# Modulation weights and their matmul visits moved from attention to the output projection, with attention's plan drawn anew

## The chip, the cores and the metric

The kernel runs on one core of one Trainium2 chip. The metric is the time of one execution on the device in microseconds, the median of several runs. Five engines work side by side, each through its own list of instructions in order: TensorE (PE, with its weight loads PEld), VectorE (DVE), ScalarE (ACT), GpSimd (POOL) and SyncE (SP), which issues nearly all DMA transfers here.

## The reference, cut to what matters

One layer of a diffusion transformer runs over 128 context tokens and 512 latent tokens with shared weights. Its second half is modulated by vectors that come out of the conditioning vectors `c` and `c_ctx`; their weights `w_ada` are what the change moves.

```python
ada_ctx = (jax.nn.silu(c_ctx) @ w_ada[i] + b_ada[i])[None, None, :]
ada_lat = (jax.nn.silu(c) @ w_ada[i] + b_ada[i])[:, None, :]
...
sh1, sc1, g1, sh2, sc2, g2 = jnp.split(ada, N_ADA, axis=-1)
u = rms_norm(h, p["g_pre1"]) * (1 + sc1) + sh1
mo, k, v = mixer(u, p, rope_tabs, ctx_k, ctx_v)
h = h + g1 * rms_norm(mo, p["g_post1"])
u = rms_norm(h, p["g_pre2"]) * (1 + sc2) + sh2
h = h + g2 * rms_norm(conv_ffn(u, p), p["g_post2"])
```

In `mixer`, attention has 16 query heads in four groups that share a key and value head each. Context tokens see only context tokens; latent tokens see all latent keys and 128 cached context keys, 640 in all. Its output is multiplied by `w_att_out` (1024 x 1024), which is the output projection of the change.

## The kernel before

All 640 tokens stay on the core. Every float32 operand of a large product is cut into a high and a low part ("hi" by ScalarE, "lo" by VectorE or GpSimd), and three matmuls replace one. Weights come as units of 512 KB into one of three `raw` buffers and are cut into one of three pairs `whi`, `wlo`. Units 8 to 15 are the query weights, two to each group; 16 and 17 are weights of two gates, 18 to 25 the eight column tiles of `w_att_out`.

Attention works in 36 steps, nine to a head group: one for the context tokens and two for each of four tiles of 128 latent tokens. `q_tile` makes the queries of one group and tile out of four pieces (`q00.0` and so on, line 689), which VectorE, ScalarE and GpSimd rotate and normalise, and which are turned on TensorE (line 1055). A step then runs as a chain:

- the scores `s` of two heads (line 1097, TensorE);
- their maximum (line 1144, VectorE), the exponential (line 1149, ScalarE), its high part `P1` (line 1155, ScalarE) and low part `P2` (line 1162 on VectorE for the first head; line 1160 for the second, on GpSimd where `POOL_WAY` has a 1, else on VectorE);
- a DMA transpose `T` of each head's parts, from `P` to `PT` (line 1166, or 1127 for the context step, SyncE);
- the product `pv` with the values (line 1191, TensorE), after a spreading of the inverse sums (line 1183);
- scaling and cutting of the result into `AH` and `AL`.

The order of all this is written out by hand. `work` names each piece of work with its engine, what it comes after and the buffers ("rooms") that it takes from a pool. `follow` then goes through the string `PLAN`: each item is the number of a piece, a letter for one of its ways (which engine does it), and digits that pick its buffers. Each engine, SyncE included, gets its instructions in the order of the plan. Behind attention, TensorE, VectorE and ScalarE keep the order of the program, while the framework places SyncE's transfers itself, as soon as their buffers allow.

The modulation weights: `w_ada` of the second scale and part of the second shift come as ten loads of 512 KB. Two of them go to `AR`, memory that attention's output will use later; eight go through the `raw` ring between the units (`LOADS`). A visit multiplies two of these loads by the conditioning vectors: `ada2_mm` issues 16 small matmuls (line 288), and VectorE adds the result to `acc`, which lies in a table no longer needed (line 1014 for the first, 1016 for the others). There are five visits in attention (`VISITS`), and `ada2_fold` (lines 315 to 321) turns `acc` into columns of `mod`, read far later, in the feed-forward half.

The projection follows directly. Its loop has eight column tiles `j`; each takes a unit, cut two tiles ahead (`next_unit`, lines 198 and 199, loads at line 215), and runs 48 matmuls (lines 233 to 235) of 320 columns into two PSUM banks, `2j` and `2j + 1` modulo 8, by way of `plain_gemm`. Beside it, in tiles 0 to 5, the list `making` builds the right-hand operands `T1` to `T4` of the next stage, and tiles 6 and 7 begin the loads of the next stage.

Of the kernel before, what the change touches and what calls it, by code (L numbers as in the profile page):

```python
# [12 lines left out]
F32 = mybir.dt.float32  # L13
# [35 lines left out]
68a0 44a0 22a00 67a 2a1 11a 32a11 23a 122a 41a 69a 14a2 121a 3a 21a 33a 123a 15a 34a1 70a 12a22 4a 24a2 31a 42a30 0a 71a 16a 6a  # L49
45a 35a 80a1 73a0 1a4 36a 74a 72a0 81a 51a1 75a 5c0 82a 7a 8a3 43a 37c1 25a 83a 9a 46a 76b 38a4 86a1 10a 93a2 139a 26a 47b2  # L50
106a0 84a10 39a 27a3 87a 48a3 40a 94a 88a 13b 49a 28a1 50a 17a4 77a4 29a 95a 78a0 30a 52a3 140b 96a 53a 18a1 79a 99a0 141b 54a3
97a22 19a 367a2 55a 100a 85a 144a 108a2 368a 101a 58b4 56a3 369a 109a 20a 89a 57a 60a1 90a1 107a 110a 371a3 370a 91a1 124a3 372a
59a0 92a 373a5 111a 98a 125a 65a 63a 102a 379a21 112a01 184a 61a 66b 185a 114a2 103a0 380a 126a1 104a2 64b 115a 381a 385a 127a
116a 382a2 105a 128a 62a 386a0 383a 113a 374a0 145a 117a 390a 384a1 392a01 375a0 147b 387a1 376a 118a4 377a 393a 129a 388a 119a3
378a 394a 398a 142a0 132a1 146b 389a0 120a 399a1 143a 133a 130a12 134a 395a3 409a21 186a 403a 400a0 396a 131a 148a 215a 410a
397a2 135a 415a 411a 149a 217b 391a1 416a0 150a2 216b 151a0 420a 412a4 422a01 152a 401a 220a 417a2 413a 158a0 423a 414a3 418a
136a4 428a 159a 424a 402a4 137a0 160a 153a 429a1 138a 187a4 425a1 154a 433a 419a5 430a3 426a 155a3 161a 431a 156a1 188a 261a
157a 439a02 427a0 164a2 162a01 404a 440a 163a 432a1 445a 441a 171a0 165a 260a 446a0 166a 172a 405a0 450a 442a4 452a12 406a 167a
447a0 443a 173a 407a 448a 458a 444a2 168a2 174a 408a 169a2 453a 459a1 421a1 449a4 170a 177a1 454a 178a 469a20 175a12 179a 460a2
463a 189a0 455a1 470a 461a 434a 475a 471a 176a 462a3 456a 476a0 190a 180a 435a1 480a 472a3 482a10 436a 457a5 477a4 473a 191a  # L60
437a 478a 488a 474a0 499a2 438a 489a 483a 192a 479a1 500a 490a0 451a1 195a0 491a 501a 464a 193a20 492a2 196a 194a 484a 181a2
502a 202a0 197a 182a3 493a 503a2 183a 203a 485a1 198a 504a 465a2 486a 199a2 505a4 221a 204a 466a 511a21 200a0 223b 467a 201a
487a3 468a 205a 222b 512a 481a1 517a 208a2 262a 513a 206a01 518a1 209a 218a0 207a 514a3 522a 210a 524a01 291a 515a 211a 219a
519a4 516a5 530a 293b 212a4 525a 494a 531a 520a 213a1 532a0 224a 214a 495a0 292b 533a 521a0 526a 263a4 496a 527a2 535a 225a 296a
264a 497a 336a 528a 541a12 337a 227a1 498a 534a1 226a1 234a1 228a 547a 229a 529a2 523a0 542a 548a 230a 235a 543a 549a1 231a2
552a 236a 232a2 550a 544a3 237a 233a 551a3 545a 554a20 240a0 241a 238a22 546a0 536a 242a 560a 239a 247a1 555a 537a1 561a0 243a
538a 248a 556a 571a10 539a 565a 557a4 540a 562a0 244a0 558a 249a 245a3 563a 572a 559a5 250a 246a 573a 577a 553a0 564a1 253a2
578a1 254a 251a00 255a 574a2 584a20 582a 579a1 575a 252a 265a1 585a 256a 576a2 580a 590a 257a3 586a 266a 258a0 566a 591a0 259a
581a0 587a3 601a10 595a 567a2 588a 592a4 267a 607a 589a3 593a 602a 268a 608a1 568a 594a1 271a1 614a20 569a 269a11 603a 272a
278a1 270a 609a0 615a 273a 604a2 612a 570a 279a 620a 616a 274a 506a0 605a 297a 610a 280a 606a5 507a0 617a1 508a 631a1 298b 621a0  # L70
618a 281a 611a4 509a 632a 299b 622a3 643a02 510a 284a0 625a 633a 623a 338a 282a22 275a0 649a 596a1 283a 276a1 634a 285a 650a1
277a 583a 286a 619a1 644a 635a4 651a2 294a0 636a 287a 597a1 624a3 652a 645a 656a21 598a 599a 654a 895a 637a0 295a 600a 657a
646a0 288a1 897b 662a 300a 653a2 289a2 658a 290a 896b 301a 647a 663a 626a1 302a0 898a 659a1 667a 303a2 613a 660a 648a1 664a3
304a 638a0 665a 627a0 305a 661a3 673a02 628a 639a2 306a 629a 640a 630a 339a3 641a 666a4 679a 307a1 642a 680a0 340a 902a 655a0
674a 906a 308a3 681a4 309a 686a12 675a 682a 930a1 676a2 684a 687a 668a 683a5 692a 688a 310a1 677a 693a1 678a0 311a 669a1 697a
689a0 670a 703a02 694a1 690a 671a 695a 312a 691a1 709a 704a 313a 710a0 696a2 672a 705a 314a10 716a12 711a3 315a 714a 323a0 316a1
722a 712a 706a4 685a1 317a 723a 717a 318a 713a3 324a 707a 724a2 718a 725a 319a 698a 708a4 719a0 727a 320a2 699a2 720a 325a 726a0
321a0 700a 733a21 322a 701a 721a5 702a 326a 739a 715a1 734a 329a0 740a1 327a21 735a 746a01 330a 328a 741a1 744a 331a 341a0 736a3
747a 332a 728a 737a 748a 742a 752a 738a1 749a4 763a2 729a0 342a 750a 753a0 743a2 764a 333a2 754a2 343a 757a 730a 334a1 751a3
755a 765a 344a 335a 775a10 345a02 756a4 731a 766a 347a2 346a 732a 767a0 354a0 781a 348a 907a1 782a1 776a 349a 355a 768a 783a3  # L80
908a 350a 777a 769a0 788a02 784a 899a 786a 356a 778a1 789a 900b 785a5 909a 794a 790a 901b 357a 779a 795a0 910a 358a11 791a4
805a12 799a 360a1 359a 792a 911a 796a2 351a0 361a 811a 903a 758a1 797a 806a 352a2 745a 812a1 780a3 353a 904b 807a 818a02 905b
798a4 813a0 816a 912a0 808a3 824a 814a 759a0 793a1 819a 913a 825a0 809a 362a 820a 914a 815a2 760a 826a1 835a21 829a 363a 761a
827a 821a2 762a 915a 841a 787a1 822a 916a 842a1 836a 364a0 828a3 843a4 848a01 365a3 844a 837a 366a 800a 823a5 849a 838a0 846a
854a 917a0 850a 845a1 839a 801a2 918a 855a0 802a 919a 810a4 803a 865a21 859a 856a1 804a 851a2 857a 920a 866a 770a1 921a 871a
867a 830a0 858a0 852a 872a1 817a 868a4 876a 853a3 873a3 869a 878a01 831a1 874a 771a0 832a 840a5 772a 833a 922a2 884a 773a 879a
875a2 885a 923a 774a 880a 834a 860a1 870a4 886a1 889a 881a2 924a 887a 931a 882a 888a0 847a 925a 883a3 861a2 862a 877a0 863a 864a
926a 927a 890a 928a 891a1 892a 893a 929a 894a
"""
POOL_WAY = "11111110100111111011101111111110"  # L90
# [20 lines left out]
def trunk_layer(ctx, tc, x_prompt, x_sample, cache_k, cache_v, c, c_ctx, w_ada, b_ada, g_pre1, g_post1, g_pre2,  # L111
# [557 lines left out]
    AR = region(ra, "r2b", [2, 1024], F32, "AR")  # L669
# [57 lines left out]
    with tc.tile_pool(name="att", bufs=1) as at:  # L727
# [16 lines left out]
        acc = both[1].rearrange("p a d -> p (a d)")[:, 0:256]  # L744
# [40 lines left out]
        def load(key, pos):  # L785
            after = [w for w in raw_users.get(ring[-3], ())] if len(ring) >= 3 else []

            def do():
                if key[0] == "a":
                    ada2_load(key[1])  # L790
                else:
                    state["limit"] = key[1] + 1
                    fetch(key[1] + 1)
            ring.append(key)
            loaded[key] = work(f"load {key}", "SP", do, after)
# [183 lines left out]
        def first_step(g, t):  # L979
# [6 lines left out]
        LOADS = [("u", 10), ("a", 0), ("a", 1), ("u", 11), ("u", 12), ("a", 4), ("a", 5), ("u", 13), ("u", 14), ("a", 6), ("a", 7), ("u", 15),  # L986
                 ("u", 16), ("a", 8), ("a", 9), ("u", 17), ("u", 18), ("u", 19)]
        VISITS = [((2, 3), 2), ((0, 1), 4), ((4, 5), 11), ((6, 7), 20), ((8, 9), 29)]
        ada_first = [work("load AR", "SP", lambda: [ada2_load(2 + i, AR[:, i]) for i in range(2)])]
        kept = []  # L990
# [4 lines left out]

        def visit(us, n):
            after = []
            for u in us:
                if u in (2, 3):
                    after += ada_first  # L1000
                else:
                    if ("a", u) not in loaded:
                        load_next(("a", u))
                    after.append(loaded["a", u])
            host = Room(ANY)

            def mm():
                ada2_mm(us, at_bank(host))
            w = work(f"ada {us}", "PE", mm, after + kept[-1:], [host])

            def keep():
                p = at_bank(host, 128)
                if us[0] == 2:
                    V.tensor_copy(acc[:, 0:128], p)
                else:
                    V.tensor_tensor(out=acc[:, 0:128], in0=acc[:, 0:128], in1=p, op=ALU.add)
            kept.append(work(f"keep {us}", "DVE", keep, [w] + kept[-1:] + (k_ready if us[0] == 2 else []), [host]))
            for u in us:
                raw_users["a", u] = [w]

        visits = {v[1]: v[0] for v in VISITS}

        def q_tile(g, t):
# [1010 lines left out]
    us = []  # L2034
# [345 lines left out]
```

## Time and profile before

| | |
|---|---|
| median of 3 runs | 1105.28 us (1102.85 to 1105.73) |
| the profiled execution | 1106.97 us |
| its span in the profile | 1105.2 us |
| attention | about 55 to 260 us |
| the output projection | about 260 to 317 us |

A row of a stage gives its start and end, its length, then for each engine the busy time and the number of instructions, and last the granted clock of TensorE (1.00 is full), the mean busy share of the 16 DMA engines and what they moved. A row in order of time gives the start, the duration, the engine, the line, the operation, output and input by the program's names, and in brackets how long the engine had been idle and what ended that. A row of waits gives who waited for whom, the total, how many times and the longest. Matmuls overlap in TensorE's pipeline, so the distance between two starts tells what one costs, and not its duration. The profile shows `acc` under the name of its table, `tabk`.

### The profile page before, as it was taken

What the parts mean: (1) busy time and instruction counts of PE and PEld (TensorE: products, weight loads), DVE (VectorE), ACT (ScalarE), POOL (GpSimd) and SP (SyncE); (2) the same over time, 40 slices, a digit from 0 to 9 for tenths busy, and PEclk for the clock granted to TensorE, in tenths of its full rate; (3) what the DMA queues carried; (4) which work ended last, traced back from release to release, by engine and by line L of the source; (5) the groups of instructions that cost most, each with busy time, mean ns of one, the idle gap of its engine ahead of it and who ended that gap; (6) DMA issues with size and microseconds to landing.
All of it is one profiled execution on the core that took longest, in us unless ns stands there. A gap on an engine that the chain in (4) does not pass through costs nothing.

```text
span 1105.2 us, 20360 instructions
## 1 busy us (share of the span) xinstructions
PE 1078.5 (98%) x8133; PEld 1001.8 (91%) x8133; DVE 856.6 (78%) x1307; ACT 584.1 (53%) x1055; POOL 135.3 (12%) x168
## 2 busy tenths in 40 slices
PE   8999988989999999999999999999999999999997
PEld 6788877879999999999999789999999999998886
DVE  5698877875559889988578558898999989989544
ACT  5468767873335445445522356655465545556442
POOL 1087545540000000000000021000000000000001
PEclk9999989999999999999999999999999999999999
DMA  9759989993234333322354645234344333435722
GB/s 322 222 134 218 180 138 187 161 180 77 77 92 122 102 95 97 106 77 77 107 185 146 214 153 153 77 100 139 110 130 127 118 108 114 127 101 190 265 85 95
DMA packets 245613, 152.18 MB, mean 138 GB/s; under 512 B 94602, under 2 KB 224134, under 8 KB 245518
## 3 DMA queue, kind: packets, MB, share of 16 engines
q1 hardware_dynamic: 245406, 150.84, 50.6%
q8 instruction: 64, 1.05, 0.4%
q14 instruction: 31, 0.25, 0.1%
q10 hardware_dynamic: 112, 0.04, 0.0%
HBM read 117.39 MB, written 11.44 MB: 117 GB/s over the span
## 4 chain that ended last, share of the span: by engine, by line
PE 87%; DMA 4%; DVE 3%; ACT 3%; issue 1%; POOL 1%; SPq 0%; DVEq 0%; ACTq 0%; POOLq 0%
PE b L1300 46%; PE b L233 10%; PE b L235 10%; PE b L234 10%; PE s L689 3%; DMA PT<-P 3%; PE s L1097 2%; PE s L1191 1%; PE s L233 1%; ACT s L1149 1%; PE s L235 1%; ACT P L1155 1%; PE s L234 1%; PE s L464 1%; DMA XT<-in_x_sample_dram 1%
## 5 line engine op out<-in xcount | busy, mean ns | idle before, releaser
L1300 PE MATMUL b<-ZBr,whi 128*128 128x320 f32 x688 | 152.1, 309 | 0.0
L1300 PE MATMUL b<-MT,whi 128*128 128x320 f32 x608 | 134.2, 309 | 0.0
L1300 PEld LDWEIGHTS b<-ZBr,whi 128*128 128x128 f32 x688 | 115.0, 188 | 0.1
L1300 PE MATMUL b<-ZBr,wlo 128*128 128x320 f32 x344 | 106.1, 309 | 0.0
L1300 PEld LDWEIGHTS b<-MT,whi 128*128 128x128 f32 x608 | 101.6, 188 | 0.0
L1300 PE MATMUL b<-MT,wlo 128*128 128x320 f32 x304 | 94.0, 309 | 0.0
L1287 ACT ACTIVATE whi<-SUM 128x1024 fp32r<-128x1024 f32 x40 | 42.2, 1054 | 78.5 <-DVE SUM L1814 76.0
L1844 DVE SCALAR_TENSOR_TENSOR Y<-C,cffn,Y 128x642 f32<-128x642 f32 x88 | 77.6, 882 | 0.9
L199 DVE TENSOR_TENSOR wlo<-raw,whi 128x1024 fp32r<-128x1024 f32 (+1 forms) x31 | 34.2, 1102 | 50.2 <-ACT whi L198 49.9
L1300 PE MATMUL b<-ZBT,whi 128*128 128x320 f32 x320 | 71.1, 309 | 0.0
L1300 PE MATMUL b<-UL,whi 128*128 128x320 f32 x228 | 70.8, 311 | 0.0
L1300 PE MATMUL b<-UH,wlo 128*128 128x320 f32 x228 | 70.1, 307 | 0.0
L1300 PE MATMUL b<-UH,whi 128*128 128x320 f32 x228 | 69.7, 306 | 0.0
L1287 ACT ACTIVATE whi<-WB 128x1024 fp32r<-128x1024 f32 x38 | 40.1, 1054 | 55.3 <-DVE WB L1395 55.3
L1291 DVE TENSOR_TENSOR wlo<-raw,whi 128x1024 fp32r<-128x1024 f32 (+1 forms) x51 | 50.4, 1019 | 21.3 <-ACT whi L1287 21.3
L1300 PEld LDWEIGHTS b<-ZBr,wlo 128*128 128x128 f32 x344 | 64.6, 188 | 0.0
L1308 ACT ACTIVATE p<-b 128x320 f32<-128x320 f32 x78 | 34.2, 439 | 55.5 <-PE b L1300 53.6
L1300 PEld LDWEIGHTS b<-MT,wlo 128*128 128x128 f32 x304 | 57.1, 188 | 0.0
L1300 PEld LDWEIGHTS b<-ZBT,whi 128*128 128x128 f32 x320 | 54.3, 188 | 1.7
L1144 DVE TENSOR_REDUCE marks<-s 128x1 f32<-128x640 f32 x64 | 51.4, 816 | 4.7 <-PE s L1097 4.7
L1291 DVE TENSOR_TENSOR wlo<-WB,whi 128x1024 fp32r<-128x1024 f32 x38 | 46.5, 1223 | 8.7 <-ACT whi L1287 8.6
L1287 ACT ACTIVATE whi<-raw 128x1024 fp32r<-128x1024 f32 (+1 forms) x51 | 43.5, 892 | 17.6 <-PE b L235 10.4
(423 smaller groups left out, 3226.8 us busy)
## 6 DMA issues: line engine op xcount, KB each, us to landing
raw<-in_w_in_dram SPq DMA_DIRECT2D x48, 512.0 KB
RAW<-in_w_up_dram SPq DMA_DIRECT2D x40, 512.0 KB
raw<-in_w_down_dram SPq DMA_DIRECT2D x22, 512.0 KB
raw<-in_w_ada_dram SPq DMA_DIRECT2D x16, 512.0 KB
actd<-Y SPq DMA_DIRECT2D x18, 321.0 KB
XT<-in_w_ada_dram SPq DMA_DIRECT2D x9, 512.0 KB
raw<-in_w_att_out_dram SPq DMA_DIRECT2D x8, 512.0 KB
raw<-in_w_conv_out_dram SPq DMA_DIRECT2D x8, 512.0 KB
```

What stands on the lines that cost most here:

```text
L199: V.tensor_tensor(out=lo[:, :n], in0=raw, in1=hi[:, :n].bitcast(F32), op=ALU.subtract)
L233: PE.matmul(out, ah, bh, start=start, stop=False)
L234: PE.matmul(out, ah, bl, start=False, stop=False)
L235: PE.matmul(out, al, bh, start=False, stop=stop)
L689: PE.matmul(out, a, b, start=start and n == 0, stop=stop and n == 2, skip_group_check=True)
L1097: PE.matmul(o[h], q_of(hl, i, rows), kk[kx][rows, g, ks], start=m == 0, stop=m == 2, tile_position=(64 * h, 0), skip_group_check=True)
L1144: V.tensor_reduce(out=mk[:, h:h + 1], in_=s_of(), axis=AX.X, op=ALU.max, negate=True)
L1287: S.activation(to[0], raw, AF.Copy)
L1291: V.tensor_tensor(out=lo, in0=raw, in1=hi.bitcast(F32), op=ALU.subtract)
L1300: PE.matmul(out, p[:, ws], q[:, k, :], start=start and k == 0 and n == 0, stop=stop and k == 3 and n == 2, skip_group_check=True)
L1308: S.activation(t, pair[j][b], AF.Copy)
L1844: V.scalar_tensor_tensor(out=y, in0=crows(j)[i][:, d:d + NACT], scalar=cffn[:, 44 * d + o:44 * d + o + 1], in1=y, op0=ALU.mult, op1=ALU.add)
```

## The change

The ten loads and the five visits leave attention, and with them `AR`, `VISITS`, `visit` and the fold. They go to the loop of the projection: four loads are issued ahead of it, into the memory of `T4` and `T2`, which `right_of` now claims only when it fills it; a visit stands behind the matmuls of tiles 0 to 4, each of the first three followed by the two loads that the buffer just read can take; the fold stands behind tile 5. `acc` moves to the end of `WB`. Attention has 912 pieces of work in place of 932, and `PLAN` and `POOL_WAY` are new; in the new plan the remaining loads (units 10 to 19) stand at other places between the transposes.

```diff
 PLAN = """
-68a0 44a0 22a00 67a 2a1 11a 32a11 23a 122a 41a 69a 14a2 121a 3a 21a 33a 123a 15a 34a1 70a 12a22 4a 24a2 31a 42a30 0a 71a 16a 6a
...
+67a0 14a0 22a00 137a 2a1 131a 44a2 15a 23a 0a 68a 3a 203a 24a0 1a1 16a 34a1 25a 6a 11a 69a 35a 41a 32a21 4a 70a 12a32 31a 21a
...
-POOL_WAY = "11111110100111111011101111111110"
+POOL_WAY = "11111111101111111011111011111110"
...
-    AR = region(ra, "r2b", [2, 1024], F32, "AR")
...
-        acc = both[1].rearrange("p a d -> p (a d)")[:, 0:256]
...
-                if key[0] == "a":
-                    ada2_load(key[1])
-                else:
-                    state["limit"] = key[1] + 1
-                    fetch(key[1] + 1)
+                state["limit"] = key[1] + 1
+                fetch(key[1] + 1)
...
-        LOADS = [("u", 10), ("a", 0), ("a", 1), ("u", 11), ("u", 12), ("a", 4), ("a", 5), ("u", 13), ("u", 14), ("a", 6), ("a", 7), ("u", 15),
-                 ("u", 16), ("a", 8), ("a", 9), ("u", 17), ("u", 18), ("u", 19)]
-        VISITS = [((2, 3), 2), ((0, 1), 4), ((4, 5), 11), ((6, 7), 20), ((8, 9), 29)]
-        ada_first = [work("load AR", "SP", lambda: [ada2_load(2 + i, AR[:, i]) for i in range(2)])]
-        kept = []
+        LOADS = [("u", u) for u in range(10, 20)]
...
-        def visit(us, n):
...
-                for n in sorted(visits):
-                    if n <= first_step(g, t):
-                        visit(visits.pop(n), n)
...
-        work("fold", "PE", folded, kept[-1:], [fold])
...
-    for name, tag in (("T1", "r5a"), ("T2", "r5b"), ("T3", "r6a"), ("T4", "r6b")):
-        z = rb.tile([128, 2, 4, HT], F32R, tag=tag, name=f"M{name}")
-        TT["m" + name] = (z[:, 0], z[:, 1])
+    TAG = {"T1": "r5a", "T2": "r5b", "T3": "r6a", "T4": "r6b"}
+    ada_rooms = {}
+
+    def ada2_fetch(i):
+        h = i // 2 % 2
+        if i % 2 == 0:
+            ada_rooms[h] = rb.tile([128, 2, 1024], F32, tag=("r6b", "r5b")[h], name=nm("ada"))
+        ada2_load(i, ada_rooms[h][:, i % 2])
...
     def right_of(name, x):
-        hi, lo = TT["m" + name]
+        z = rb.tile([128, 2, 4, HT], F32R, tag=TAG[name], name=f"M{name}")
+        hi, lo = TT["m" + name] = (z[:, 0], z[:, 1])
...
+    acc = WB[:, 3200:3328]
+    for i in range(4):
+        ada2_fetch(i)
     for j in range(KT):
         unit = next_unit()
...
                 S.activation(MA[:, j, b0:b1], out, AF.Copy)
+        if j < 5:
+            p = ada2_mm((2 * j, 2 * j + 1), bank((2 * j + 4) % 8 if j else 2))
+            if j == 0:
+                V.tensor_copy(acc, p)
+            else:
+                V.tensor_tensor(out=acc, in0=acc, in1=p, op=ALU.add)
+            if j < 3:
+                for i in (2 * j + 4, 2 * j + 5):
+                    ada2_fetch(i)
+        elif j == 5:
+            ada2_fold(acc, bank((2 * j + 4) % 8))
```

More of the change, by code (lines that the diff above doesn't have):

```diff
@@ L48 @@
 PLAN = """
-68a0 44a0 22a00 67a 2a1 11a 32a11 23a 122a 41a 69a 14a2 121a 3a 21a 33a 123a 15a 34a1 70a 12a22 4a 24a2 31a 42a30 0a 71a 16a 6a
-45a 35a 80a1 73a0 1a4 36a 74a 72a0 81a 51a1 75a 5c0 82a 7a 8a3 43a 37c1 25a 83a 9a 46a 76b 38a4 86a1 10a 93a2 139a 26a 47b2
-106a0 84a10 39a 27a3 87a 48a3 40a 94a 88a 13b 49a 28a1 50a 17a4 77a4 29a 95a 78a0 30a 52a3 140b 96a 53a 18a1 79a 99a0 141b 54a3
-97a22 19a 367a2 55a 100a 85a 144a 108a2 368a 101a 58b4 56a3 369a 109a 20a 89a 57a 60a1 90a1 107a 110a 371a3 370a 91a1 124a3 372a
@@ L53 @@
[L53 to L88, printed above, removed]
+67a0 14a0 22a00 137a 2a1 131a 44a2 15a 23a 0a 68a 3a 203a 24a0 1a1 16a 34a1 25a 6a 11a 69a 35a 41a 32a21 4a 70a 12a32 31a 21a
@@ new lines @@
+33a 45a 79a1 72a0 51a0 5a0 80a 132a 13a 8a2 7a 73a 52a3 46a 81a 17b1 9a 53a 82a 134b 10a 54a3 71a0 85a1 92a2 133a 74a 55a 56a0
+83a11 209a 93a 75a 57a 42a42 84a 76a3 94a 77a0 58b1 26a 18a1 43b 95a 78a 19a 27a2 86a 347a2 20a 98a2 105a0 87a 348a 47b3 28a3
+349a 36a 106a 88b 59b3 89a1 107a 99a 37a4 90a1 350a 29a 91a 108a 96a20 351a0 60a4 30a 48a1 111a0 118a2 112a 97a 65a 352a 38a3
+49a 113a 66a 119a 353a5 63a 50a 61a 64b 120a 109a01 39a 138a 121a 40a 110a 359a21 62a 100a 124a1 204a 114b 140a 115a1 135a0 360a
@@ new lines @@
+101a 116a2 139b 117a 361a 136a 125a 365a 102a1 206b 275a 362a2 141a 122a12 103a3 366a0 142a 126a 104a 205a 354a1 144a2 363a 123a
+281a 367a4 372a01 143a0 127a 355a0 364a0 145a 356a 146a 128a4 378a 357a 151a0 129a0 147a 358a 379a1 152a 130a 368a 373a 389a21
+380a3 370a 374a 381a 369a1 148a1 395a 153a 375a1 390a 149a1 154a 382a2 396a0 376a 157a0 150a 391a 402a10 377a3 155a21 397a0 400a
+383a 156a 158a 371a1 392a2 408a 398a 403a 164a0 409a1 393a 159a 404a 399a4 165a 410a4 413a 419a02 160a 405a3 394a5 411a 384a
@@ new lines @@
+406a 425a 407a0 161a3 385a2 166a 420a 162a3 426a0 386a 167a 412a1 163a 387a 421a 432a21 388a 168a10 427a1 430a 401a1 169a 433a
+170a1 422a0 428a 438a 434a 177a0 423a 439a1 429a2 178a 171a 435a2 443a 172a 449a01 440a3 436a 424a3 173a 414a 455a 441a 437a4
+450a 456a0 174a4 179a 175a2 415a1 176a 457a4 180a 416a 442a5 462a12 417a 458a 181a02 451a 418a 183a2 463a 431a1 452a1 182a 459a0
+453a 464a 190a0 468a 465a0 454a1 479a0 184a 469a1 466a 444a 185a 480a 470a2 467a2 186a 491a21 473a 445a0 460a 481a 446a 471a
@@ new lines @@
+191a 497a 447a 482a 472a3 492a 192a 483a3 498a0 448a 193a 484a 493a 187a1 485a4 194a21 504a10 188a0 499a4 502a 189a 195a 196a0
+461a1 505a 500a 494a1 510a 506a 474a 495a 501a5 511a 207a0 197a 475a2 515a 198a 507a0 476a 496a0 208a 477a 508a 512a2 199a 478a
+210a 521a21 509a1 513a 276a 211a 486a1 527a 212b 514a2 200a2 487a0 522a 201a1 277b 213a 528a1 488a 202a 214a 489a 875a 278b
+529a3 490a 534a10 215a1 523a 530a 879a 216a1 503a1 532a 524a4 535a 531a3 540a 536a 516a 525a 541a0 223a0 217a 517a1 545a 218a
@@ new lines @@
+542a1 518a 551a20 526a4 519a 537a0 219a 520a 224a 557a 543a 220a1 552a 225a 558a1 538a 221a3 544a0 226a 559a2 222a 564a01 229a2
+560a 553a 539a5 227a02 533a1 565a 554a3 228a 570a 566a 561a1 236a0 555a 571a0 237a 230a 567a4 562a 575a 231a 581a21 556a2 572a1
+568a 232a 546a 582a 573a 569a3 587a 583a 233a2 238a 547a0 234a2 548a 588a1 239a 235a 574a4 549a 594a01 240a21 584a0 550a 589a2
+241a 585a 563a1 242a0 590a 595a 586a0 611a2 600a 596a 249a0 591a5 612a 601a0 576a 243a 597a3 592a 605a 244a 602a4 598a 250a
@@ new lines @@
+577a2 245a 613a 599a1 578a 623a10 603a 251a 579a 629a 615a1 604a2 580a 252a 630a1 616a 246a1 255a1 624a 617a3 636a20 247a0 631a0
+253a10 625a 632a 642a 593a0 626a2 248a 637a 606a 643a 254a 633a4 634a 256a 638a 627a 262a1 257a 607a1 647a 628a0 614a 644a3 608a
+263a 258a 609a 645a 639a4 259a3 264a 610a 260a1 646a5 640a 282a 618a0 261a 653a02 284a 641a1 619a2 620a 283b 265a 621a 659a 883a
+622a 660a0 654a 279a0 268a2 666a12 876a 266a00 269a 267a 655a 635a1 672a 270a 661a1 877a 648a 656a0 667a 271a 673a1 280a 878b
@@ new lines @@
+664a 657a 649a1 674a2 272a4 650a 658a2 285a 662a 273a3 651a 274a 668a 286a 652a 887a 675a 683a02 288a0 677a 663a3 669a3 287a2
+289a 295a1 684a 290a 888a0 689a 685a 291a 296a 676a0 670a 690a0 889a 686a4 694a 696a12 691a0 687a 671a4 692a 297a 697a 292a2
+702a 698a 298a 688a1 890a 293a2 299a12 699a1 294a 891a 301a1 300a 700a 703a1 693a5 308a1 302a 892a 707a 713a01 704a2 303a 678a0
+304a 719a 705a 714a 720a0 665a 701a0 715a 726a21 679a0 706a4 724a 716a3 680a 309a 732a 681a 721a4 682a 310a 733a 717a 722a 305a0
@@ new lines @@
+311a 727a 718a2 306a0 734a0 743a0 307a 314a2 735a 695a0 728a 723a3 312a01 729a1 708a 744a 313a 736a1 730a 745a 321a1 315a 737a
+755a12 316a 731a5 709a2 746a 747a2 710a 322a 317a 761a 711a 712a 323a 762a1 756a 318a0 324a 748a 763a3 319a1 768a20 749a0 764a
+325a20 757a 320a 327a0 766a 758a4 738a0 774a 326a 765a4 769a 775a0 725a 759a 770a 750a1 328a 760a1 739a1 779a 329a 771a0 740a
+785a01 751a2 772a 741a 330a 776a1 742a 773a5 331a4 791a 777a 334a0 332a3 786a 792a1 335a 333a 778a2 787a 752a 798a12 793a2 796a
@@ new lines @@
+336a 753a 804a 794a 880a 754a 337a 805a0 799a 881b 795a3 767a1 338a10 788a3 806a4 789a 882b 780a 340a1 800a 790a0 341a 807a
+815a20 781a1 809a 801a0 782a 893a0 342a 339b 808a1 783a 816a 884a 894a 821a 343a 817a 885b 784a 895a 822a1 802a 344a1 886b 896a
+818a1 803a4 826a 345a2 828a10 819a 823a2 346a 897a 820a2 824a 797a1 834a 829a 835a0 898a0 825a5 830a 845a20 836a3 839a 810a
+831a4 846a 837a 832a 847a 899a 851a 833a0 811a2 900a 848a0 812a 901a 852a1 849a 838a3 813a 858a10 856a 853a1 814a 902a 854a
@@ L89 @@
+850a1 827a1 864a 859a 865a 903a2 855a4 860a 840a 866a2 869a 861a4 867a 904a 841a1 862a 911a 868a2 905a 842a 843a 863a5 906a 844a
+857a0 907a 908a 870a 909a 871a0 872a 873a 910a 874a
 """
-POOL_WAY = "11111110100111111011101111111110"
+POOL_WAY = "11111111101111111011111011111110"
 def rope_tables():
@@ L994, in load_next @@
                 load(LOADS[len(ring)], len(ring) - 28 if len(ring) < 3 else -5 + 2 * len(ring))
-        def visit(us, n):
[L997 to L1021, printed above, removed]
         def q_tile(g, t):
@@ L1246, in trunk_layer @@
                 users_of.setdefault(17, []).append(glast)
-        fold = Room(banks(6, 7))
-        def folded():
-            ada2_fold(acc, at_bank(fold))
-        work("fold", "PE", folded, kept[-1:], [fold])
         work("sigmoid", "ACT", lambda: S.activation(warm, mhalf[:, 0:1], AF.Sigmoid), exps_all)
```

## Prediction

> **What bounds the kernel now.** I read the page first (busy shares, chain), then the table by stage, then TensorE in order of time where attention stands still, then SyncE's queue there.
>
> ```profile
> span 1105.2 us, 20360 instructions
> PE 1078.5 (98%) x8133; PEld 1001.8 (91%) x8133; DVE 856.6 (78%) x1307; ACT 584.1 (53%) x1055; POOL 135.3 (12%) x168
> PE 87%; DMA 4%; DVE 3%; ACT 3%; issue 1%; POOL 1%; SPq 0%; DVEq 0%; ACTq 0%; POOLq 0%
> ...
> 55.00:260.00 205.00, 187.91 (x2458) 165.05 (x2457) 159.01 (x345) 152.10 (x354) 115.99 (x113) 0.98 0.91 167
> 80.00:245.00 165.00, 149.56 (x2032) 131.07 (x2034) 128.05 (x279) 126.81 (x293) 95.07 (x93) 0.98 0.99 176
> 260.30:316.70 56.40, 56.39 (x384) 56.40 (x385) 32.03 (x29) 18.95 (x26) 0.00 (x0) 1.00 0.25 74
> ```
>
> The stage rows give start:end, length, busy time of PE, PEld, DVE, ACT and POOL, granted clock, share of the 16 DMA engines, GB/s. Over the whole program TensorE is the bound, at 98%. Attention (55 to 260) is the exception: TensorE idles 205.0 - 187.9 = 17.1 us there, VectorE and ScalarE are at 78% and 77% of the inner stretch, and the DMA engines at 0.99. The projection (260.3 to 316.7) is the reverse: TensorE never idles, the DMA engines are at 0.25. So the change takes work from a stage with four nearly full resources to one with a single full resource, and that one is TensorE. From 316.7 on the next stage is as full of matmuls; I let a shift at that point pass to the end unchanged.
>
> Where attention stands still:
>
> ```profile
> PE s L1191 <- DMA PT<-P: 9.7, 5, 3.2
> ...
> 138.23 0.28 PE L689 MATMUL s<-whi,UH 128*128 128x256 f32 x1
> ...
> 139.18 0.28 PE L689 MATMUL s<-whi,UL 128*128 128x256 f32 x1
> ...
> 144.31 1.81 PE L1191 MATMUL s<-PT,VV 128*64 128x128 f16 x30 [3.20 <-DMA PT<-P]
> ...
> 146.43 0.42 PE L689 MATMUL s<-wlo,UH 128*128 128x256 f32 x1
> ...
> 148.57 0.41 PE L689 MATMUL s<-whi,UL 128*128 128x256 f32 x1
> ...
> 185.56 1.03 PE L1191 MATMUL s<-PT,VV 128*64 128x128 f16 x30 [2.61 <-DMA PT<-P]
> ...
> 243.85 1.03 PE L1191 MATMUL s<-PT,VV 128*64 128x128 f16 x30 [2.39 <-DMA PT<-P]
> ...
> 140.00:150.00 10.00, 6.80 (x67) 6.04 (x65) 4.79 (x11) 3.43 (x8) 2.58 (x4) 0.66 0.78 126
> ...
> 180.00:190.00 10.00, 7.01 (x135) 5.79 (x132) 5.63 (x15) 4.79 (x11) 2.30 (x3) 1.00 1.14 196
> ...
> 240.00:250.00 10.00, 7.61 (x110) 6.83 (x112) 5.16 (x12) 6.66 (x16) 1.75 (x2) 0.83 1.16 188
> ```
>
> The one large wait is that of the values' product (L1191) for a transposed tile: five waits, 9.7 us, three of them long. They cost more than their length. Behind the first, eight matmuls that took 0.95 us before it (138.23 to 139.18, 0.119 each) need 0.214 each (ten in 146.43 to 148.57): TensorE runs at half clock from 144.3 to about 149.6, which loses 2.6 us. The window at 240 has 0.83 of the clock, a loss of 10 x 0.17 = 1.7. Behind the second the clock stayed at 1.00. The waits with their clock cost 9.7 + 2.6 + 1.7 = 14.0 us.
>
> What the transposes stand behind, in SyncE's queue:
>
> ```profile
> 85.75 1.37 SPq L1166 DMA_TRANSPOSE PT<-P  x1
> ...
> 132.95 1.24 SPq L215 DMA_DIRECT2D raw<-in_w_in_dram  x2
> 134.29 0.52 SPq L282 DMA_DIRECT2D raw<-in_w_ada_dram  x1
> 134.90 4.52 SPq L1166 DMA_TRANSPOSE PT<-P  x1
> ...
> 177.72 0.62 SPq L215 DMA_DIRECT2D raw<-in_w_in_dram  x1
> 178.51 2.28 SPq L1166 DMA_TRANSPOSE PT<-P  x1
> ...
> raw<-in_w_ada_dram SPq DMA_DIRECT2D x6, 512.0 KB
> raw<-in_w_att_out_dram SPq DMA_DIRECT2D x4, 512.0 KB
> PT<-P SPq DMA_TRANSPOSE x64
> ```
>
> A transpose takes 1.37 us to issue when the queue is clear, 4.52 behind three loads, 2.28 behind one. The first two long waits, at 144.3 and 185.6, follow exactly these two places; the third has no load near it. A load is 524,288 bytes. The projection's row moves 74 GB/s at a share of 0.25, so 296 GB/s when full, 1.77 us a load. Between 80 and 245 there are 16 loads (six of them moved by the change, four of w_att_out and six of w_in), 28.3 us; the other 0.99 x 165 - 28.3 = 135 us belong to 64 transposes, 2.1 us each. The six loads that leave free 6 x 1.77 = 10.6 us of a queue that is full. The page "DMA: Bandwidth & Descriptors" of the Trainium skill (Latency and other measured facts) gives 261 GB/s for a transpose; for its 327,680 bytes that is, as an estimate from that page, 1.26 us, and the DMA engines would be only two thirds full. The share of 0.99 speaks against it, and the measurement decides; what would follow if the engines do have room is the second rival.
>
> **The change part by part.** First what leaves attention.
>
> ```profile
> 180.68 1.08 PE L288 MATMUL s<-raw,s 128*32 128x128 f32 x32
> 181.70 0.44 PE L1055 MATMUL s<-ident,QF 128*128 128x128 f32 x2
> ...
> 187.60 0.41 PE L315 MATMUL s<-sel,tabk 128*128 128x32 f32 x2
> 187.94 0.44 PE L1183 MATMUL s<-ident,marks 128*64 128x128 f32 x4
> ...
> 188.05 0.17 DVE L319 TENSOR_TENSOR mod<-s,feat 128x16 f32<-128x16 f32 x1 [4.21 <-PE s L315]
> ...
> L1014 DVE COPY tabk<-s x1: 293/293/293, 78.8 to 78.8; 128x128 f32<-128x128 f32 x1
> ```
>
> A visit occupies TensorE from 180.68 to 181.70, 1.02 us; five are 5.1. The fold takes 187.60 to 187.94, 0.34. Work of 5.4 us leaves a TensorE that is 91% busy; between nothing (they sat in idle time) and 5.4 I take 5.4, because work stands directly before and behind each. VectorE loses five small sums and the fold, and with it the 4.2 us that it stood still for the fold while TensorE waited for a transpose. I count nothing for that: the same transpose held both. By the new plan's way letters it does six half cuts more and two P2 fewer, so it stays about as full.
>
> Second, the waits. I counted in both plans how many score steps stand between a step's scores and its values' product in TensorE's order. Before, ten steps from 10 to 32 have two or fewer (10 to 13, 18 to 20, 22 to 24) while others have up to eight; after, five have two (11, 18, 20, 27, 29) and nearly all others three or four. The waits at 144.3 and 185.6 belong to steps 11 and 19, both with two; the one at 243.9 to step 30, whose transpose stood behind one of step 32, and after stands in turn. The loads that remain also move: u13 to u15 go ahead of step 1's transposes, u16 and u17 behind step 11's transposes, u18 and u19 on either side of one of step 21; none waits for a buffer whose last cut stands behind it. Half of the short distances are gone, and I let half of the 14.0 go: -7.0. Bounds: all 14.0 go, or none.
>
> Against that, the softmax starts later: the last query tile of the first group now stands before step 1. Its 24 matmuls at 0.119 are 2.85 us, and the two visits that stood there, 2.04, are gone: +0.8. Attention: -5.4 - 7.0 + 0.8 = -11.6.
>
> Third, the projection. The visits come back one for one, 5.1, and the fold 0.34, on an engine with no idle time. New is a wait behind the first visit: its sum is copied out of bank 2, and the next tile's matmuls begin in that bank. The fold's row gives 188.05 - 188.01 = 0.04 us from TensorE's end to VectorE's start; a drain of 0.28, that hop twice and a copy of 0.29 make 0.65. TensorE stands for it; VectorE's next cut waits behind the copy, and it is needed only a tile later. Later visits use banks whose next tile is two tiles away, and the fold reads a sum finished a tile before: nothing. Together +6.1; bounds 5.4 and, with a 0.65 at each visit, 8.7.
>
> Fourth, the loads in the projection, at nothing:
>
> ```profile
> 250.75 3.10 SPq L1166 DMA_TRANSPOSE PT<-P  x2
> ...
> 257.33 1.01 PE L1191 MATMUL s<-PT,VV 128*64 128x128 f16 x30
> ...
> 260.31 0.38 PE L233 MATMUL b<-AHa,whi 128*128 128x320 f32 x1
> ...
> 291.46 22.90 SPq L1380 DMA_DIRECT2D raw<-in_w_in_dram  x4
> ...
> DMA  9995000000000000002699991000000000000006
> ```
>
> A tile of the projection is 56.4 / 8 = 7.05 us, so the first visit comes at 260.3 + 7.05 = 267.4. Its loads go to memory that attention's tiles hold, at worst until the last values' product ends, 258.3. The last line is the DMA share in 40 slices of 286 to 300: the load issued at 291.46 is over by slice 25, 294.8, 3.3 us later. Two loads from 258.3 land by 258.3 + 3.3 + 1.8 = 263.4, four microseconds early, room for two loads of w_att_out ahead of them. The later ones are issued two tiles before their visit, 14 us. On the queue they pass, a load that waits for a visit holds back loads of w_att_out, which are wanted a tile later still. The DMA engines go from 0.25 to 0.25 + 17.7 / 62 = 0.54. The four loads taken from before 80 leave a stretch where the DMA wasn't full.
>
> Sum: -11.6 + 6.1 = -5.5. The profiled execution took 1106.97 us (span 1105.2 and 1.8 around it), 1.7 over the median of 1105.28; a shift carries over, so 1105.28 - 5.5 = 1099.8, and 1101.5 if profiled like before.
>
> **The rivals.** *The softmax sets attention's pace (slower).* Nothing in attention gets shorter: each step goes through a maximum, an exponential, two parts and a transpose on engines at 77 to 99%, the visits filled idle time, and the waits only change place. Then the 6.1 is added bare: 1111.4. It decides once attention shrinks by less than 6.1. For it: 17.1 us of idle TensorE, VectorE and ScalarE at 78 and 77%. Against: waits of known cause are more than half of that idle time.
>
> *Attention shrinks by its visits alone (about even).* The transposes' lateness comes from the steps before them and the DMA engines have room, so taking loads away frees nothing: -5.4 + 0.8 + 6.1 = +1.5, 1106.8. For it: the third long wait has no load near it.
>
> *The first visit waits for its loads.* If four or more loads go ahead, or the memory comes free only after attention's last instruction, TensorE stands before the second tile. Priced by the wait at 144.3 and its clock, 3.2 + 2.6 = 5.8, it makes 1105.6. Against: the four microseconds above. The page "TensorE: Matmul & The Clock Gate" (Part 1: The HAM clock gate) says that the clock halves after an idle window of about 3.4 us that runs free of the kernel; here 3.20 and 2.39 us halved it and 2.61 did not, so length alone doesn't say.
>
> **How the numbers follow.** Forecast 0.55, with a range of its own from 1094 (most of the waits go) to 1103; even 0.20; softmax's pace 0.17; late loads 0.08. The range for 8 in 10 takes in the slower case: 1094 to 1111.5. A measurement of this kernel can tell about 0.3%, 3.3 us. Faster by more: nearly all of the forecast, 0.51. Within it: the rest of it, half of the even case and of the late loads, 0.04 + 0.10 + 0.04 = 0.18. Slower: the softmax's case and the other halves, 0.31.
>
> **What would show it.** Right: the last score step and the projection's first matmul come some 11 us sooner, the wait of L1191 for transposes falls to about half, no transpose takes over 3 us to issue, the projection lasts 62.5 us with one gap of 0.6 before its second tile. Wrong: attention shorter by under 6 us, new waits of L1191 or of the scores in attention, or a wait of L288 for a load.

## The result, and the profile after

The changed kernel takes 1097.14 us (1096.69 to 1097.35), the kernel before, beside it, 1105.51: a ratio of 0.9927, 95% interval 0.991 to 0.9945, so 8.4 us less. On another chip the ratio was 0.9936 (0.9923 to 0.995). The forecast was 5.5 us less.

The stages of both kernels. Attention is counted here from the first matmul of the first query tile to the first of the projection, the projection from there to the first matmul of the next stage. First the table by stage of the kernel before:

```profile
58.57:260.31 201.74, 184.63 (x2443) 162.19 (x2442) 155.64 (x336) 149.45 (x350) 115.99 (x113) 0.97 0.91 165
260.31:316.80 56.49, 56.49 (x385) 56.49 (x385) 32.03 (x29) 18.94 (x26) 0.00 (x0) 1.00 0.25 74
```

Then that of the changed kernel:

```profile
57.95:243.14 185.19, 175.92 (x2282) 155.23 (x2280) 155.49 (x338) 145.75 (x340) 111.24 (x106) 0.99 0.83 152
243.14:306.44 63.30, 62.79 (x547) 60.82 (x547) 34.01 (x37) 18.95 (x26) 0.00 (x0) 1.00 0.57 150
...
140.00:150.00 10.00, 9.31 (x125) 8.05 (x123) 8.26 (x18) 8.64 (x21) 5.30 (x6) 1.00 1.20 192
180.00:190.00 10.00, 10.00 (x141) 9.16 (x141) 6.88 (x16) 7.31 (x18) 5.13 (x5) 1.00 1.06 183
240.00:250.00 10.00, 9.85 (x89) 9.52 (x89) 5.35 (x6) 4.00 (x6) 0.00 (x0) 1.00 0.76 193
```

Attention is 16.55 us shorter, the projection 6.81 longer. It begins 0.62 earlier, and what follows takes 0.46 more (1095.3 - 306.44 against 1105.2 - 316.80). Together -9.9, the difference of the spans (1105.2 to 1095.3); the profiled executions differ by 9.8 (1106.97 to 1097.14). The medians differ by less, 8.4, since the profiled execution of before is 1.5 us above its median. Attention's 16.55 split into 7.84 of idle TensorE (17.11 to 9.27) and 8.71 of busy time (184.63 to 175.92). The visits and the fold are 5.4 of the latter, and the clock fits the rest: the windows of 10 us below 1.00 lose 3.4 + 1.7 = 5.1 us before (0.66 and 0.83, in the prediction's rows) and 1.7 after. The three windows that were at 6.8, 7.0 and 7.6 busy, two of them with a lowered clock, are at 9.3, 10.0 and 9.85, all at 1.00; the third of them now lies mostly in the projection.

TensorE's waits in the changed kernel (who waited for whom, total, times, longest),

```profile
PE s L1151 <- DMA PT<-P: 2.3, 4, 0.7
PE s L1018 <- DVE AL L1173: 1.2, 3, 0.6
```

and in order of time the head of the projection, first SyncE's row, then TensorE's:

```profile
242.14 3.95 SPq L281 DMA_DIRECT2D ada<-in_w_ada_dram  x4
...
243.14 0.38 PE L232 MATMUL b<-AHa,whi 128*128 128x320 f32 x1
...
250.12 0.31 PE L234 MATMUL b<-AHb,wlo 128*128 128x320 f32 x1
250.36 1.08 PE L287 MATMUL b<-ada,s 128*32 128x128 f32 x32
251.94 0.39 PE L232 MATMUL b<-AHa,whi 128*128 128x320 f32 x1 [0.51 <-DVE WB L1474]
252.17 0.31 PE L233 MATMUL b<-AL,whi 128*128 128x320 f32 x1
...
258.92 0.31 PE L234 MATMUL b<-AHb,wlo 128*128 128x320 f32 x1
259.16 1.08 PE L287 MATMUL b<-ada,s 128*32 128x128 f32 x32
260.17 0.42 PE L232 MATMUL b<-AHa,whi 128*128 128x320 f32 x1
260.43 0.31 PE L233 MATMUL b<-AL,whi 128*128 128x320 f32 x1
```

The values' product (now L1151) waits 2.3 us for transposes in place of 9.7, and 0.7 at most. (One sign of the prediction failed beside that: a transpose at 135.28, behind two loads, took 3.17 us to issue, where none was to take over 3.) The four first loads are issued just before the projection begins, and the visit at 250.36 waits for none. A visit between two tiles takes more than its 1.02 us: from 258.92 to 260.43 is 1.51, less two steps of 0.147 makes 1.22. The first, with the wait for bank 2, makes 252.17 - 250.12 - 0.294 = 1.76. Four times 1.22, 1.76 and the fold make up the 6.81.

### The profile page after: what moved, and what is told of

The parts are those of the page before. It is cut to its first block, busy times and chain, and to the rows that moved or that the text cites. A ratio compares the mean times of both kernels' runs of the same rounds, so it can differ in the third digit from the quotient of the medians.

```text
span 1095.3 us, 20378 instructions
## 1 busy us (share of the span) xinstructions
PE 1075.9 (98%) x8133; PEld 998.4 (91%) x8133; DVE 858.6 (78%) x1316; ACT 580.9 (53%) x1047; POOL 130.4 (12%) x161
## 4 chain that ended last, share of the span: by engine, by line
PE 78%; ACT 1%; DVE 1%; DMA 0%; SPq 0%; issue 0%; POOL 0%; DVEq 0%; ACTq 0%
PE b L1255 46%; PE b L232 10%; PE b L234 10%; PE b L233 10%; PE b L1874 1%; DMA PT<-P 0%; PE b L287 0%; SPq L1126 0%; PE b L1724 0%; DVE marks L1104 0%; ACT P L1115 0%; ACT E L1109 0%; PE s L687 0%; PE b L350 0%; ACT s L1109 0%
```

## The experiments

Three theories: the new order carries the gain, by the distance from scores to values' product (A); the loads that leave a full DMA queue carry it (B); the visits sat in idle time and their removal is worth nothing (the rival of the softmax's pace). The prediction's even case, that the visits alone count and the loads free nothing, is answered by the same runs. The plan can be redrawn piece by piece, since each is named; in the variants below each engine keeps its order except for what is said. The table gives attention's length as above, from one profiled execution each, and the ratio of the times to the kernel before, from several runs. Attention of the changed kernel, profiled three times, lasted 185.19, 185.58 and 185.45 us (after, after_again, after_bank). The times of the kernels with the old order spread by up to 5 us, so a difference of one or two us between their lengths is not resolved. Each is told below.

| kernel | order | loads in attention | visits in attention | attention us | ratio (95%) |
|---|---|---|---|---|---|
| before | old | ten | five | 201.74 | 1 |
| old_loads | old | eight | none | 198.61 | 1.0049 (1.0033 to 1.0065) |
| old_visits | old | none | five | 197.38 | 1.0043 (1.0027 to 1.0059) |
| old_order | old | none | none | 197.22 | 1.0040 (1.0025 to 1.0055) |
| new_loads | new | eight | none | 191.13 | 1.0002 (0.9988 to 1.0016) |
| new_visits | new | none | five | 191.11 | 0.9990 (0.9981 to 1.0000) |
| after | new | none | none | 185.19 | 0.9927 (0.991 to 0.9945) |

All but the kernel before also have the loads and visits in the projection, which takes 63.3 us in each.

**old_order**: the change without its new order.

```diff
-PLAN, POOL_WAY: those of the changed kernel
+PLAN, POOL_WAY: those of before, without "load AR", the eight loads ('a', i), the five "ada" and "keep", and "fold"
```

> The change without its new order: loads and visits are in the projection, but attention's plan and its ways are those of before with the twenty pieces of the loads and visits taken out. Theory A (the order carried most of the gain: short distances from scores to values' product made the waits): the waits of the values' product for transposes stay near the 9.7 us of before, attention is only some 5 to 9 us shorter than before, the time is 1101 to 1105, ratio 0.996 to 1.000. Theory B (ten loads less in a full DMA queue carried it): waits fall to 2 to 4 us, attention 13 to 17 us shorter, 1097 to 1100, ratio 0.993 to 0.995.

It is slower than before by 0.4%, 1107.85 us: theory B fails. Its stage row, and then its waits:

```profile
57.90:255.12 197.22, 179.67 (x2281) 157.74 (x2280) 153.62 (x329) 149.04 (x350) 115.94 (x113) 0.97 0.81 144
```

```profile
PE s L1151 <- DMA PT<-P: 5.1, 5, 2.2
PE s L1018 <- POOL QF L865: 2.4, 2, 1.7
PE s L894 <- DVE PT L855: 1.8, 1, 1.8
PE s L1057 <- DVE P L1085: 1.3, 1, 1.3
```

The DMA engines went from a share of 0.91 to 0.81, the wait for transposes from 9.7 to 5.1, and TensorE's idle time stayed: 197.22 - 179.67 = 17.6 against 17.1. Other waits took the place, for query tiles from GpSimd and for key tiles. Attention lost 4.5 us, the projection gained 6.8. A's ranges were missed too, for the time, for the waits (5.1 in place of some 9.7) and for attention (5 to 9 us shorter): even less came than it said. By the ratio the time grew by 4.4 us (2.8 to 6.1), which with 6.8 in the projection leaves some 2.4 for attention by the medians, in place of the 4.5 of this execution.

**new_loads**: the changed kernel with loads back.

```diff
+    AR = region(ra, "r2b", [2, 1024], F32, "AR")
+        for i in range(8):
+            work(f"spare load {i}", "SP", lambda i=i: ada_load(AR[:, i % 2], ...))
```

> The changed kernel with eight loads of 512 KB put back into attention at about the places of before, into memory that nothing reads; the projection keeps its ten. Theory A: the new order leaves room, +0 to +3 us over the 1097.1 of the changed kernel, waits of the values' product under 5 us. Theory B: six loads in the full stretch cost 1.77 us each, +7 to +11 us, 1104 to 1108, waits back near 10 us.

**new_visits**: the changed kernel with visits back. They read `UH`, and stand after step 1 and later, since their sum's table is free only then.

```diff
+            for h in range(2):
+                ada_mm(at_bank(sroom, 128), UH...[:, (i + h) * 512:(i + h) * 512 + 1024].bitcast(F32), ...)
+            ... "spare keep" on VectorE behind each, "spare fold" behind step 22
```

> The changed kernel with five more visits and a fold in attention, on data that is there anyway, with no loads; the projection keeps its own. Theory A (TensorE sets attention's pace, visits cost what they occupy): +5 to +6 us, 1102 to 1103. Rival (the softmax sets the pace and visits fill idle time): +0 to +1.5 us, 1097 to 1098.6.

Loads cost 5.9 us of attention, visits 5.9. The stage row of new_loads and its longest wait:

```profile
57.73:248.86 191.13, 174.57 (x2281) 153.95 (x2280) 156.09 (x338) 145.95 (x340) 111.22 (x106) 1.00 0.91 169
```

```profile
PE s L1152 <- DMA PT<-P: 8.7, 7, 2.0
```

The stage row of new_visits, and its wait for transposes:

```profile
57.57:248.68 191.11, 178.56 (x2444) 157.93 (x2442) 158.01 (x346) 145.89 (x340) 111.93 (x106) 1.00 0.81 147
```

```profile
PE s L1151 <- DMA PT<-P: 1.1, 2, 0.9
```

With loads, the wait for transposes is back at 8.7 us and TensorE idles 16.6. With visits, the busy time grows by 2.6, the idle time by 3.3, and the wait for transposes stays away. Neither cost hangs on the clock, which was 1.00 in both: in after_bank (below), with the same plan as the changed kernel and a clock of 1.00 too, attention is 185.45, and 5.7 us are left for each. By the ratios the loads cost 7.3 to 8.3 us and the visits 6.0 to 7.0 (against after_again and after), give or take 2.5. So in the new order both cost: the loads more than A's three and, by the ratios, what B said; the visits about what theory A said, though part of it is new idle time and not their own work.

**old_loads** and **old_visits**: the same pieces put back into old_order, at their places of before.

> The kernel old_order (plan of before, loads and visits in the projection) with eight loads put back into attention at their places of before, into memory that nothing reads. Two theories of why loads and visits together brought the old order only 4.5 us of attention (201.7 to 197.2). A: in the old order the loads' delay of the transposes is what counted and the visits sat in idle time: +3 to +5 us over old_order's 1107.9, attention near 201. B: the visits counted and the loads hardly: +0 to +1.5 us.

> The kernel old_order with five visits and a fold put back into attention at their places of before, on data that is there anyway, and no loads. A (visits sat in idle time): +0 to +1.5 us over 1107.9. B (TensorE's work counted): +3 to +5.5 us, attention near 201.

The stage rows of old_loads and old_visits:

```profile
58.18:256.79 198.61, 180.44 (x2282) 158.60 (x2280) 153.71 (x329) 149.77 (x350) 115.95 (x113) 0.97 0.88 162
58.45:255.83 197.38, 182.66 (x2443) 159.91 (x2442) 155.34 (x336) 148.81 (x350) 115.94 (x113) 0.99 0.85 144
```

In the old order the loads cost 1.4 us of attention and the visits 0.2; by time, both ratios lie within the interval of old_order's, and the costs are 1.0 and 0.3 us, give or take 2.4. So the loads cost less than A here said in this execution, but by time its three us are not excluded. The visits' 5.4 us of work were met in two ways: TensorE idles 2.8 us less (14.7 against 17.6), as the rival had it, and its matmuls ran at a higher clock (0.99 over attention in place of 0.97: one window of 10 us at 0.83, a loss of 1.7 us, against windows at 0.94, 0.89 and 0.66 in old_order, 5.1). Whether the filled idle time kept the clock up is not shown. In the new order five such visits cost 5.9.

**new_short** and **old_long**: the distance itself.

```diff
-... 's6' 'pv3' ... 's7' 'pv4' ...
+... 'pv3' 's6' ... 'pv4' 's7' ...      (new_short: 23 steps of the new order)
-... 's13' 'pv11' ... 's14' ...
+... 's13' ... 'pv11' 's14' ...         (old_long: 10 steps of old_order, with their scaling and cutting)
```

> The changed kernel with 23 of the values' products moved one score step earlier in TensorE's order, so that most stand two steps behind their scores in place of three. Theory A (distance makes the waits): the waits of L1151 for transposes go from 2.3 us to over 15 us and the time rises by 10 us or more, over 1107. Theory B (the loads made the waits, and with them gone two steps are enough): +0 to +4 us, waits under 6 us.

> The kernel old_order with the ten values' products that stood two steps behind their scores (10 to 13, 18 to 20, 22 to 24) moved one step later, their scaling and cutting with them. If the short distances made the old order slow: the long waits of L1151 go, 5 to 10 us less than 1107.9, attention 187 to 192. If something else of the new order counts (the spread of loads, cuts and score steps, the first group's query tile, the ways): within 2 us of 1107.9, or slower.

new_short takes 1128.7 us (ratio 1.0223, 1.0206 to 1.024), attention 219.2. Its waits:

```profile
PE s L1143 <- DVE AL L1173: 9.4, 5, 3.2
PE s L1057 <- ACT E L1109: 5.6, 6, 2.0
PE s L1143 <- DVE QT L1022: 5.0, 5, 1.3
...
PE s L1151 <- DMA PT<-P: 1.7, 2, 0.9
```

The time is as A said, the wait isn't: TensorE stands at the first instruction of a values' product (L1143), behind VectorE, and hardly ever at the transposed tile itself. old_long took the wait for transposes from 5.1 to 2.1 us, and attention became no shorter for it, 200.1 against 197.2 (ratio 1.0063, 1.004 to 1.0086; by time it can't be told from old_order). So distances made shorter cost much, 34 us of attention, but by waits for VectorE; and distances made longer remove the waits for transposes without making attention shorter. A's mechanism, waits for transposes that come of short distances, is not borne out.

**new_long_bank**: the five short distances of the new order made three, and another bank for the first visit.

```diff
-            p = ada2_mm((2 * j, 2 * j + 1), bank((2 * j + 4) % 8 if j else 2))
+            p = ada2_mm((2 * j, 2 * j + 1), bank((2 * j + 4) % 8))
```

> The changed kernel with its five short distances (steps 11, 18, 20, 27, 29) lengthened to three, and the first visit in the projection given bank 4 in place of 2, so that the second tile need not wait for the copy. If distance is still what is left: 1 to 3 us less than 1097.1, wait for transposes below 1 us; the bank takes 0.5 us off the projection (63.3 to 62.8). If not: 1096.6 within a microsecond, only the bank's half microsecond seen in the trace.

It takes 1105.74 us (1.0013, 1.0003 to 1.0024). Attention is 195.8, 10.7 longer: the wait for transposes falls to 1.5, and waits for the low part's cut out of the bank (L1173) take over. Of the 10.7, 1.7 stand ahead of step 1, where the plan is still that of the changed kernel: step 1 begins 26.1 us after attention in place of 24.4 (84.40 - 58.29), with a clock of 0.84 from 70 to 80 in this execution.

```profile
PE s L687 <- DVE AL L1173: 3.9, 2, 2.1
PE s L1143 <- DVE AL L1173: 1.8, 2, 1.6
PE s L1151 <- DMA PT<-P: 1.5, 2, 0.8
```

By these rows a later values' product holds its PSUM bank longer, and the next query tile (L687) wants it; this was not tested further. (The lengthened plan also had to choose eleven buffers anew.)

**after_again** and **after_bank**, side by side on another chip; the second has the diff of the bank alone.

> The changed kernel once more, beside the kernel before on the same chip, for the comparisons below: both theories expect 1097 us within a microsecond, a ratio near 0.993, and again some 9 us of idle TensorE in attention against 17 before.

> The changed kernel with the first visit in bank 4 in place of bank 2, nothing else. If the second tile waits for the copy out of bank 2 alone: the 0.51 us of idle ahead of it goes, the projection takes 62.75 us in place of 63.30, the time falls by 0.5 us, to 1096.6. If it then waits for something else (the next bank, the loads), no change.

1097.70 and 1096.89 us (ratios 0.9936 and 0.9933, 0.9919 to 0.9947): they can't be told apart by time. In the trace the wait is gone, 0.55 us of the projection (the stage rows of after_bank, attention and projection, and its first visit in order of time):

```profile
58.04:243.49 185.45, 174.77 (x2282) 154.34 (x2280) 156.09 (x338) 145.62 (x340) 111.42 (x106) 1.00 0.82 152
243.49:306.24 62.75, 62.75 (x547) 60.81 (x547) 33.91 (x37) 18.94 (x26) 0.00 (x0) 1.00 0.57 150
```

```profile
250.70 1.08 PE L287 MATMUL b<-ada,s 128*32 128x128 f32 x32
251.71 0.42 PE L232 MATMUL b<-AHa,whi 128*128 128x320 f32 x1
```

**new_old_ways** and **new_old_cuts**: the new order with the old sharing of work between VectorE and GpSimd.

```diff
-POOL_WAY = "11111111101111111011111011111110"
+POOL_WAY = "11111110100111111011101111111110"    (new_old_ways alone)
-... 133a ... 140a ... 205a ... 211a ... 284a ... 877a     (six "lo" pieces, VectorE)
+... 133b ... 140b ... 205b ... 211b ... 284b ... 877b     (both: GpSimd)
```

> The changed kernel's order with the ways of before for the low parts: the old POOL_WAY, and all the half cuts on GpSimd that were there before. If the new sharing between VectorE and GpSimd carried much of the new order's gain: 5 us or more over 1097.1, with new idle of TensorE. If the sequence itself carried it: within 2 us of 1097.1.

> The changed kernel with six half cuts of weights given back from VectorE to GpSimd, as before, and nothing else: order, buffers and POOL_WAY stay. If the sharing of the cuts carried the loss of new_old_ways (9.3 us of attention): attention 192 to 195 in place of 185.2, 1104 to 1107 us. If it was the ways of P2, or the reshuffling of buffers that they needed: within 2 us of 1097.1.

new_old_ways loses 9.3 us of attention (194.5) and all of the gain (1107.16, ratio 1.0017, 1.0006 to 1.0029). Of the 9.3, 2.9 are lost ahead of step 1 (85.25 - 57.93 = 27.3 in place of 24.4), with a clock of 0.70 from 70 to 80. The six cuts alone lose 2.4 (187.6; 1099.23, ratio 0.9953, 0.9936 to 0.9969), which by time is not clear of after_again's 0.9936. The rest of the 9.3 belongs to `POOL_WAY`, to the four buffers and the two pieces at other places that came with it in the plan (491 and 534), or to that clock; these weren't told apart.

## Why the prediction was right, and where it was not

- **The sum.** -8.4 us for a forecast of -5.5, inside its range. Both halves were too small: attention lost 16.55 in place of 11.6, the projection gained 6.81 in place of 6.1. As in the result, 1.5 of the difference of the profiles is the slower profiled execution of before.
- **The waits, half of 14.0.** The term was mis-sized: 7.4 of the 9.7 us of waits went, and both clock losses with them, 11.7 of the 14.0. (The first loss was taken as 2.6; counted as the second was, from its window's 0.66, it is 3.4.) The only lowered clock left is a new one at 60 to 70.
- **The start of the softmax, +0.8.** It was +3.0: step 1 begins 24.4 us after attention (82.36 - 57.95) in place of 21.4 (80.00 - 58.57). The lowered clock from 60 to 70, shown last, makes no difference to it: in after_bank, with the same plan and a clock of 1.00 there, step 1 begins 24.45 us after attention (82.49 - 58.04). VectorE is busy 9.4 to 9.9 of every 10 us from 60 to 80 in both; that it sets this start was not tested. The rows of the changed kernel and of after_bank:

```profile
82.36 0.93 PE L1057 MATMUL s<-KH,QT 64*128 64x320 f32 x2
82.49 0.90 PE L1057 MATMUL s<-KH,QT 64*128 64x320 f32 x2
```

- **The distance as the cause.** This step failed. The count of steps pointed to the right waits, and the better plan is more even, but lengthening distances made the new order slower and the old one no faster, and shortening them brought waits for VectorE in place of waits for transposes.
- **The loads.** The issue times and the first two waits pointed at them, and in the old order the wait for transposes did fall by half without loads and visits; attention hardly gained. In the new order they count: 5.9 us in one execution, 7.3 to 8.3 by the ratios, for six loads in the full stretch 1.0 to 1.4 each, not 1.77. The share of 0.99 was read as DMA engines that are full. The rows shown with it have 1.14 and 1.16, and the changed kernel has 1.20 from 140 to 150, so the share can pass 1 and does not say how much room is left; it does not speak against the second rival.
- **The visits, -5.4.** Taken as independent of the order. They were worth 0.2 in the old order, 5.9 in the new one, each with the loads already gone. The rival of the softmax's pace, with 0.17, described the old order in the main: with loads and visits moved and nothing else, attention paid back 4.5 and the projection charged 6.8. The rival of the visits alone fits neither order: in the old one they were worth nothing that can be told, in the new one the loads cost as well. The forecast came true through the plan, with which TensorE idles 9.3 us in attention in place of 17.1; for this term that was luck, since nothing in the prediction made the visits' worth depend on the order.
- **The projection, +6.1.** The wait for bank 2 was 0.51 to 0.55, 0.65 forecast; the visits were under-priced at 1.02 from a row where each stood among short products, and took 1.22 between tiles. The loads were hidden, as forecast.

What in the new order does it, beyond the sharing of work between VectorE and GpSimd (2.4 us for six cuts in one execution), stays open: order alone is worth 12.0 us with loads and visits out (197.22 to 185.19), 7.5 with the loads in and 6.3 with the visits in. No move by hand within attention's order, in either of the two, made it faster. So a plan drawn for just these pieces may also lose by a piece put in, whatever it is; no run tells this from the cost of the loads and visits as such.

## What to carry to other kernels

In a stage where several engines are nearly full, a piece taken away can be worth nothing until the order is drawn anew around the gap: five visits cost 0.2 us in one order and 5.9 in another. Price such a removal by the idle time that is left after it, and test it with the old order before believing the sum. Price work that moves to a dense stage from rows where it stands between the same neighbours, its weight loads and bank included.

## What the runs showed of the hardware that was not expected

TensorE's clock was lowered to 0.83 in the changed kernel's window from 60 to 70, in which it idled 1.66 us in all and the longest single wait was 0.93:

```profile
60.00:70.00 10.00, 8.34 (x65) 7.18 (x64) 9.40 (x17) 3.25 (x7) 8.79 (x10) 0.83 0.17 51
```

after_bank, with the same plan for attention, shows the same window at full clock:

```profile
60.00:70.00 10.00, 7.39 (x67) 6.39 (x66) 9.78 (x19) 3.31 (x8) 8.80 (x10) 1.00 0.18 56
```

The prediction had seen waits of 3.20 and 2.39 us lower it; in old_order it fell to 0.66 in the window from 180 to 190 with one of 2.19. after_again shows 0.83 from 60 to 70 once more, new_visits and new_loads 1.00, and new_long_bank, with the same plan up to there, 0.84 from 70 to 80, so a profile of one execution can show such a drop or not, and at one place or another. Nor does it always cost time: attention lasts 185.19 us with the drop at 60 to 70 and 185.45 without it. The idle window of about 3.4 us that "TensorE: Matmul & The Clock Gate" of the Trainium skill (Part 1: The HAM clock gate) states for the drop was not reached by any of these single waits.
